# All engines of a hybrid token-mixing block in program order, its weight stages in one stream

## The chip, the cores and the metric

The kernel runs on one core of one Trainium2 chip. The metric is the device time of one execution in microseconds; runs before the change took 1920.9, 1925.97 and 1927.42 us, and their median, 1925.97 us, is the time before. Engines are named as in the profile: PE (TensorE), PEld (its weight loads), DVE (VectorE), ACT (ScalarE), POOL (GpSimd), SP (SyncE, which issues the DMAs here).

## The reference

One layer of a block over 256 latent tokens `x` and 256 context tokens `ctx` of width 2048, in float32. A conditioning vector gives six modulation rows (shift, scale, gate for the mixer and for the feed-forward part) through `w_ada`, 2048 x 12288. The mixer's input is a modulated RMSNorm; one input projection `w_in` feeds three branches and their gates:

```python
h = _rmsnorm(x, norm_mix_w) * (1 + sc_m) + sh_m       # context likewise, with its own modulation
u = h @ w_in                  # x, B, C, dt of the SSD | z | pool | Fourier | 3 gates
y = sum(gate_i * branch_i)    # box pooling, 2-D DFT, bidirectional Mamba-2 SSD
x = x + g_m * (y @ w_out)
h2 = _rmsnorm(x, norm_ffn_w) * (1 + sc_f) + sh_f
x = x + g_f * ((silu(h2 @ w_gate) * (h2 @ w_up)) @ w_down)
out = _rmsnorm(x, final_norm_w)
```

The lines above are the reference in short form. `D_FF` is 5632. The SSD runs in chunks of 128 over four groups of eight heads; `B` and the convolved columns of `x` come from 512 tokens (latent and context).

## The kernel before, in words

Float32 matrix products are made from two rounded parts of each operand, a high and a low one: `split` casts the high part on ACT (line 124) and subtracts for the low part on DVE (line 125), and `mm3` issues three PE products (lines 143 to 145, mostly 128x512). Weights stream through SBUF in stages of two k-tiles, 128x2x512 elements or 512 KB: a load into one of four `raw` buffers, a split into one of three `whi` and `wlo` pairs, then 12 products for a token-major projection. A few such stages per output, written as `proj` (line 595), make up most of the program: 8 per 512 columns of `w_in`, `w_ssd_out`, `w_out`, `w_ffn_gate` and `w_ffn_up`, 4 or 8 for `w_fourier` and `w_ffn_down`.

The first phase goes over eight row slices, `quanta`. For each, 64 PE records form 512 columns of the mixer's modulation from eight 512 KB tiles of `w_ada` (line 262), `adasb` (266) and `L269` turn them, `Am` and `Sm` (276 to 278) take them, `xnT` (287) applies them to two k-tiles of the normed tokens, and `hh`, `hl` are the parts of the result. With them go B (512 columns of `w_in`), the first 256 columns of x and dt, whose accumulators stay in PSUM over all eight slices. The other columns of x follow later (`project_x`), then C, z, the pooling input, the Fourier input, the SSD, the gates and the branches' outputs, in the order of the string `ORDER`.

The rest of the modulation (`ada_rest`, line 344: scale and shift of the feed-forward part, SC_F and SH_F, and the gates G_M, G_F) isn't made on PE but on DVE, as units: load 512 KB of `w_ada`, 128x1024, into one of the `raw` buffers, multiply by the column of `sil` and add to `adacc` (lines 353, 355). After 16 units `adacc` is split, and eight narrow products (with `strip`), a copy and a transpose, or two products with a row of ones, put it where it is used. `bg(n)` pulls these units, a set fraction of one per stage; lines 851 and 852 pull what is left of SC_F, SH_F and G_M ahead of `w_out`. G_F's units come under the SwiGLU's first stages.

What sets the order: on SP it is that of the program up to the end of the first phase, and later loads are tied to the last weight load. PE, DVE and ACT are held in program order in the input norms; PE also in the last 512 columns of `w_out`, where the norm of one token tile is made under the products of the other (`stage_h`, `norm_ffn`, `turn`). Everywhere else a list scheduler puts the instructions of an engine in order, by dependences and the program's place. Buffers in rings come free in the order of their use.

Of the kernel before, what the change touches and what calls it, by code (L numbers as in the profile page):

```python
# [64 lines left out]
WORK_AT = (0, 1, 8)  # L65
FETCH, STAGE, AT_W = 8, 1, 4

QR, QE = 4, 1
APART, APART2, TURNS0, TURNS1 = 3, 3, 1, 1
ORDER = "u P x0 c x1 u s0 x2 s1 z0 F x3 P z1 s2 p0 F z2 p1 f0 s3 z3 p2 f1 Y f2 p3 q0 f3 q1 q2 q3"  # L70
BG = {"x": 0.5, "z": 0.5, "u": 0.5, "p": 0.35, "F": 0.35, "f": 0.35, "q": 0.35, "s": 0.45}
# [3 lines left out]
def hybrid_block(ctx: ExitStack, tc, io):  # L75
# [10 lines left out]
    hp = pool("hp", 30)  # L86
    qp = pool("qp", 8)
    psp = pool("psp", 4, space=bass.MemoryType.PSUM)

    in_order = tc.manual_schedule(engines={mybir.EngineType.SP})  # L90
    in_order.__enter__()
    names = [0]
    last = [None]

    def load(dst, src):
        with tc.issue_after(last[0].ins):
            nc.sync.dma_start(dst, src)


    def nm(s):  # L100
        names[0] += 1
        return f"{s}{names[0]}"

# [5 lines left out]

    def TB(shape, nme="t"):  # L110
        return H(shape, nme=nme)
# [15 lines left out]
    def stage_raw(src, n=CH):  # L127
        raw = wp.tile([P, 2, n], F32, tag="raw", name=nm("raw"), bufs=4)
        last[0] = nc.sync.dma_start(raw, src)
        return raw  # L130

    def stage(src, n=CH, raw=None):
        raw = raw or stage_raw(src, n)
        hi = wp.tile([P, 2, n], F32R, tag="hi", name=nm("whi"), bufs=3)
        lo = wp.tile([P, 2, n], F32R, tag="lo", name=nm("wlo"), bufs=3)
        split(hi, lo, raw)
        return hi, lo

# [8 lines left out]
    # ---------------------------------------------------------------- constants  # L147
    pp = C([P, PP_N], nme="pp")
    cc = C([P, CC_N], nme="cc")
    nc.sync.dma_start(pp, io["pp"])  # L150
# [10 lines left out]
    for t in range(4):  # L161
        src = (x if t < 2 else cx)[(t % 2) * P : (t % 2 + 1) * P, :]
        halves = [H([P, 1024], nme="xt") for _ in range(2)]
        for i, h in enumerate(halves):
            nc.sync.dma_start(h, src[:, i * 1024 : (i + 1) * 1024])
        tok.append(halves)
        if t == 0:
            nc.sync.dma_start(cc, io["cc"])

    sil = C([P, 32], nme="sil")  # L170
# [4 lines left out]
    stat = H([P, KT, 32], nme="stat")  # L175
# [14 lines left out]
    # ---------------------------------------------------------------- input norms  # L190
# [3 lines left out]
    def scale_rows(t):  # L194
        r = rst[:, t : t + 1]
        ssq = C([P, 2], nme="ssq")
        for i in range(2):
            S.activation(H([P, 1024], nme="junk"), tok[t][i], AF.Square, accum_out=ssq[:, i : i + 1])
# [19 lines left out]
    with tc.manual_schedule(engines={mybir.EngineType.PE, mybir.EngineType.DVE, mybir.EngineType.Activation}):  # L218
        S.activation(C([P, 1], nme="pre"), pp[:, 0:1], AF.Square)
        S.activation(C([P, 1], nme="pre"), eps, AF.Sqrt)  # L220
        for t in range(4):
            scale_rows(t)
            if t:
                turn_in(t - 1)
        turn_in(3)
        S.copy(ones_r, ONE)
        S.copy(gt_r, GT)
        S.copy(lt_r, LT)

    # ---------------------------------------------------------------- modulation of the mixer, B and dt  # L230
# [3 lines left out]
    hl = [None] * 8  # L234

    bacc_ = [acc() for _ in range(4)]
    xacc0 = [aux() for _ in range(2)]
    dtps = aux()

    raws, w_raw = [], []  # L240

    def fetch(upto):
        while len(raws) < min(upto, 64):
            j, i = len(raws) // 8, len(raws) % 8
            raws.append(H([P, 4, 256], nme="raw"))
            nc.sync.dma_start(raws[-1], rows(w_ada, 4 * (i % 4), 4, i // 4 * D + j * 256, 256))

    def modulation(j, work):
        ps = aux()

        def units(i):
            for _ in range(WORK_AT.count(i)):
                next(work, None)

        for i in range(8):
            if i == AT_W:
                w_raw.append([stage_raw(rows(w_in, 2 * j, 2, c0, n), n) for c0, n in ((B_OFF, CH), (0, 256))])
            fetch(8 * j + i + FETCH)
            p = i % 4
            o = slice(i // 4 * 256, (i // 4 + 1) * 256)  # L260
            for k in range(4):
                T.matmul(ps[32 * k : 32 * k + 32, o], stat[:, 4 * p + k, :], raws[8 * j + i][:, k, :],  # L262
                         start=p == 0, stop=p == 3)
            units(i)
        sb = Q([P, CH], nme="adasb")
        S.copy(sb, ps)
        units(8)
        for i in range(4):
            T.matmul(ps[:, 2 * i : 2 * i + 2], sb[:, i * P : (i + 1) * P], SEL, start=True, stop=True)  # L269
# [5 lines left out]
        r = ps[:, 0:8].rearrange("p (a b) -> p a b", b=2)  # L275
# [4 lines left out]
    def modulate(b):  # L280
        hh[b] = H([P, 2, CH], F32R, nme="hh")
        hl[b] = H([P, 2, CH], F32R, nme="hl")
        for k in range(2):
            kt = 2 * b + k
            for s in range(2):
                v = xnT[b][:, k, s * 256 : (s + 1) * 256]
                V.tensor_scalar(v, v, Am[:, kt, s : s + 1], Sm[:, kt, s : s + 1], ALU.mult, ALU.add)
            split(hh[b][:, k, :], hl[b][:, k, :], xnT[b][:, k, :])

    def project_bc(b):  # L290
        """B, dt and the first columns of x of quantum b, in steps"""
        hi, lo = stage(None, CH, w_raw[b][0])
        xhi, xlo = stage(None, 256, w_raw[b][1])
        yield

        def part(out, h, l, cs):
            for k in range(2):
                kt = 2 * b + k
                mm3(out, h[:, k, cs], l[:, k, cs], hh[b][:, k, :], hl[b][:, k, :], kt == 0, kt == KT - 1)

        for ct in range(4):
            part(bacc_[ct], hi, lo, slice(ct * P, (ct + 1) * P))
            yield
        for k in range(2):
            kt = 2 * b + k
            w = dtp[kt // 8][:, kt % 8, :]
            T.matmul(dtps, w, hh[b][:, k, :], start=kt == 0, stop=False)
            T.matmul(dtps, w, hl[b][:, k, :], start=False, stop=kt == KT - 1)
        yield
        for ct in range(2):  # L310
            part(xacc0[ct], xhi, xlo, slice(ct * P, (ct + 1) * P))
            yield

    work = iter(())
    fetch(8)
    dtw = H([P, KT, 64], nme="dtw")
    nc.sync.dma_start(dtw, rows(w_in, 0, KT, DT_OFF, 64))
    # the parts of the columns of dt side by side: upper, lower
    dtp = [H([P, 8, P], F32R, nme="dtp") for _ in range(2)]
    for i in range(2):  # L320
        split(dtp[i][:, :, 0:64], dtp[i][:, :, 64:128], dtw[:, 8 * i : 8 * i + 8, :])
    for j in range(8):
        modulation(j, work)
        for _ in work:
            pass
        work = project_bc(j)
        if STAGE == 0:
            next(work)
        modulate(j)
        if STAGE == 1:  # L330
            next(work)
    for _ in work:
        pass

    in_order.__exit__(None, None, None)

    # ---------------------------------------------------------------- background: rest of the modulation
# [6 lines left out]
    def ada_rest(offs):  # L344
        for off in offs:
            for half in range(2):
                a = wp.tile([P, 1024], F32, tag="adacc", name=nm("adacc"), bufs=1)
                for kt in range(KT):
                    raw = wp.tile([P, 1024], F32, tag="raw", name=nm("raw"), bufs=4)
                    c0 = off + half * 1024  # L350
                    load(raw, w_ada[kt * P : (kt + 1) * P, c0 : c0 + 1024])
# [4 lines left out]
                    yield  # L356
                hi = wp.tile([P, 1024], F32R, tag="hi", name=nm("whi"), bufs=3)
                lo = wp.tile([P, 1024], F32R, tag="lo", name=nm("wlo"), bufs=3)
                split(hi, lo, a)
                if off in (SC_F, SH_F):  # L360
                    ps = aux()
                    for i in range(8):
# [29 lines left out]
    def bg(n):  # L392
        owed[0] += n
        while owed[0] >= 1:
            owed[0] -= 1
            next(rest, None)
# [744 lines left out]
```

## Time and profile before

| | |
|---|---|
| Runs: median (lowest to highest) | 1925.97 us (1920.9 to 1927.42) |
| Profiled execution, span | 1922.6 us |
| HBM read | 405.56 MB, 212 GB/s over the span |
| PE matmul records | 8804 |

For the profiled execution the span is the time that is listed; its distance to the median of the runs is 3.4 us. The profile has a page (busy time per engine, chain of waits, costliest groups) and views that can be asked for a window, a tile or a line. In a row of instructions, `out<-in` are the program's names, `L125` is the line of the kernel, and the number behind the bar is the busy time in us followed by the mean of one in ns. Times in the timeline are start and duration in us.

### The profile page before, as it was taken

To read this page: it belongs to the slowest core of one execution; us is meant where nothing else is said; L and a number is where in the kernel's file an instruction comes from. 1 tells how busy PE (TensorE), PEld (TensorE's weight loads), DVE (VectorE), ACT (ScalarE), POOL (GpSimd) and SP (SyncE) were. 2 spreads that over 40 slices of the span, in tenths; PEclk is the share of its full clock that TensorE was granted. 3 is DMA by queue.
4 is the path that set the end of the run, shared out by engine and by line. 5 is a ranking of instruction groups with operands and counts; after the bars stand their busy time and mean duration, and the time that the engine had idled before them with its cause. 6 is when DMAs were issued, how large, how long until landed. Compare 5 with 4: busy or idle time off the path is not lost.

```text
span 1922.6 us, 23276 instructions
## 1 busy us (share of the span) xinstructions
PE 1847.1 (96%) x8804; PEld 1483.4 (77%) x8804; DVE 1236.8 (64%) x1515; ACT 852.5 (44%) x1177; POOL 0.2 (0%) x4
## 2 busy tenths in 40 slices
PE   5999999999999999999999999999999999999998
PEld 3677886867777768777877887787788888888886
DVE  4338869695886687766656657666655555555567
ACT  5225535464464454533434544443343444433444
POOL 0000000000000000000000000000000000000000
PEclk8999999999999999999999999999999999999999
DMA  9985745454656747677777665787766666656655
GB/s 333 353 288 158 243 145 167 142 155 158 186 157 208 248 152 252 216 250 247 244 248 245 201 226 152 256 277 260 247 211 191 196 188 186 191 192 196 187 186 175
DMA packets 214081, 409.19 MB, mean 213 GB/s; under 512 B 14801, under 2 KB 51793, under 8 KB 213969
## 3 DMA queue, kind: packets, MB, share of 16 engines
q1 hardware_dynamic: 213968, 407.71, 67.1%
q8 instruction: 69, 1.13, 0.3%
q14 instruction: 44, 0.35, 0.1%
HBM read 405.56 MB, written 2.10 MB: 212 GB/s over the span
## 4 chain that ended last, share of the span: by engine, by line
PE 66%; DMA 17%; DVE 11%; issue 4%; ACT 2%; DVEq 0%; SPq 0%; ACTq 0%
PE acc L144 19%; PE acc L145 19%; PE acc L143 19%; DMA raw<-w_ada 14%; DVE wlo L125 5%; DVE adacc L355 2%; PE aux L262 1%; DVE cv L407 1%; PE aux L560 1%; DMA t<-ptab 1%; PE aux L522 1%; DMA raw<-w_in 1%; ACT whi L124 1%; PE aux L759 1%; DMA psc<-pool_scale 1%
## 5 line engine op out<-in xcount | busy, mean ns | idle before, releaser
L124 ACT CAST whi<-raw 128x1024 fp32r<-128x1024 f32 (+1 forms) x553 | 574.2, 1040 | 799.5 <-PE acc L145 554.2
L125 DVE TENSOR_TENSOR wlo<-raw,whi 128x1024 fp32r<-128x1024 f32 (+1 forms) x553 | 662.3, 1207 | 354.2 <-ACT whi L124 353.3
L144 PE MATMUL acc<-wlo,h2h 128*128 128x512 f32 x704 | 275.4, 391 | 2.5 <-DVE wlo L125 2.5
L143 PE MATMUL acc<-whi,h2h 128*128 128x512 f32 x704 | 275.0, 391 | 2.3 <-ACT h2h L124 2.3
L145 PE MATMUL acc<-whi,h2l 128*128 128x512 f32 x704 | 275.4, 391 | 0.0
L355 DVE SCALAR_TENSOR_TENSOR adacc<-raw,sil,adacc 128x1024 f32<-128x1024 f32 x120 | 154.0, 1283 | 176.1 <-DMA raw<-w_ada 175.8
L144 PE MATMUL acc<-wlo,lh 128*128 128x512 f32 x512 | 201.8, 394 | 5.4 <-DVE wlo L125 5.4
L143 PE MATMUL acc<-whi,lh 128*128 128x512 f32 x512 | 201.3, 393 | 0.0
L145 PE MATMUL acc<-whi,ll 128*128 128x512 f32 x512 | 200.6, 392 | 0.0
L144 PEld LDWEIGHTS acc<-wlo,h2h 128*128 128x128 f32 x704 | 132.4, 188 | 30.9 <-DVE wlo L125 3.8
L143 PEld LDWEIGHTS acc<-whi,h2h 128*128 128x128 f32 x704 | 132.3, 188 | 29.6 <-ACT h2h L124 2.7
L145 PEld LDWEIGHTS acc<-whi,h2l 128*128 128x128 f32 x704 | 132.5, 188 | 28.2 <-DVE h2l L125 1.3
L145 PE MATMUL acc<-whi,al 128*128 128x512 f32 x320 | 124.7, 390 | 0.0
L144 PE MATMUL acc<-wlo,ah 128*128 128x512 f32 x320 | 124.7, 390 | 0.0
L143 PE MATMUL acc<-whi,ah 128*128 128x512 f32 x320 | 124.6, 389 | 0.0
L144 PEld LDWEIGHTS acc<-wlo,lh 128*128 128x128 f32 x512 | 96.1, 188 | 29.9 <-DVE wlo L125 9.9
L145 PE MATMUL acc<-hh,wlo 128*128 128x512 f32 x288 | 113.8, 396 | 0.8 <-DVE wlo L125 0.8
L144 PE MATMUL acc<-hl,whi 128*128 128x512 f32 x288 | 114.5, 398 | 0.0
L143 PE MATMUL acc<-hh,whi 128*128 128x512 f32 x288 | 112.1, 402 | 0.9 <-ACT whi L124 0.9
L143 PEld LDWEIGHTS acc<-whi,lh 128*128 128x128 f32 x512 | 96.1, 188 | 20.7 <-issue 0.8
L145 PEld LDWEIGHTS acc<-whi,ll 128*128 128x128 f32 x512 | 96.1, 188 | 19.8 <-issue 0.2
L145 PEld LDWEIGHTS acc<-whi,al 128*128 128x128 f32 x320 | 60.1, 188 | 12.4
(294 smaller groups left out, 2467.8 us busy)
## 6 DMA issues: line engine op xcount, KB each, us to landing
raw<-w_in SPq DMA_DIRECT2D x200, 512.0 KB, 4.6
raw<-w_ada SPq DMA_DIRECT2D x192, 512.0 KB, 5.1
raw<-w_ffn_gate SPq DMA_DIRECT2D x88, 512.0 KB, 4.4
raw<-w_ffn_up SPq DMA_DIRECT2D x88, 512.0 KB, 4.4
raw<-w_ffn_down SPq DMA_DIRECT2D x88, 512.0 KB, 4.1
raw<-w_ssd_out SPq DMA_DIRECT2D x32, 512.0 KB, 4.9
raw<-w_out SPq DMA_DIRECT2D x32, 512.0 KB, 4.2
raw<-w_fourier SPq DMA_DIRECT2D x16, 512.0 KB, 4.5
```

Source lines behind the costliest of these rows:

```text
L124: S.copy(hi, src)
L125: V.tensor_tensor(lo, src, hi.bitcast(F32), ALU.subtract)
L143: T.matmul(out, ah, bh, start=first, stop=False)
L144: T.matmul(out, ah, bl, start=False, stop=False)
L145: T.matmul(out, al, bh, start=False, stop=last)
L262: T.matmul(ps[32 * k : 32 * k + 32, o], stat[:, 4 * p + k, :], raws[8 * j + i][:, k, :], start=p == 0, stop=p == 3)
L355: V.scalar_tensor_tensor(a, raw, sil[:, kt : kt + 1], a, ALU.mult, ALU.add)
L407: V.scalar_tensor_tensor(o[:, :, a:b], src[:, :, a + d : b + d], w[k], o[:, :, a:b], ALU.mult, ALU.add)
L522: T.matmul(ps, btk[:, 2 + t, :], xc[d][t], start=t == 0, stop=t == 1)
L560: T.matmul(seg, m, rh, start=n == 0, stop=n == 3)
L759: T.matmul(ps[:, k, :], u_pool[c][:, t, cc_ * P : (cc_ + 1) * P], tb[:, i, t, :], start=t == 0, stop=t == 1)
```

## The change

All engines now issue in program order (`tc.manual_schedule()` without a list). The program first lists `Stage`s, one for each 512 KB of weights with a function for its products, and `stream` then walks through them: loads are issued up to seven stages ahead, splits up to two, then come the stage's products, and behind them segments of side work, taken from generators in `beside` until the stage's `room` (1.45 us by the program's own cost figures) is used. `need` runs a generator to its end on the spot.

```diff
+LEAD, RAWS, PARTS = 2, 5, 3
+HS, QS = 28, 15
...
+    def need(*keys):
+
+        for key in keys:
+            while key not in ended:
+                step(next(e for e in beside if e[0] == key))
+
+    def stream():
+        while at["run"] < len(stages):
+            i = at["run"]
+            st = stages[i]
+            load_upto(i + LEAD + RAWS)
+            split_upto(i + LEAD + 1)
+            if st.first:
+                st.first()
+            st.mm(st.parts)
+            room = st.room
+            for entry in list(beside):
+                while room > 0.25:
+                    cost = step(entry)
+                    room -= abs(cost)
+                    if cost >= 0:
+                        break
+            for f in st.after:
+                f()
+            at["run"] += 1
```

The first phase has three stages per slice: B and two groups of 512 columns of x. Products of x end in PSUM after each slice and are added up in SBUF by DVE. The modulation of the next slice (`ada_tile`) is spread over the groups of the B and x0 stages, and `modulate` stands at the start of x1:

```diff
+    def stage_x(j, g):
+        def mm(parts):
+            if g == 1:
+                modulate(j + 1)
+            for ct in range(4):
+                ps = aux()
+                feature(ps, parts, j, ct * P, True, True)
+                if j == 0:
+                    x_sum[g, ct] = Q([P, 2, 256], nme="xin")
+                    S.copy(x_sum[g, ct].rearrange("p a b -> p (a b)"), ps)
+                else:
+                    v = x_sum[g, ct].rearrange("p a b -> p (a b)")
+                    V.tensor_tensor(v, v, ps, ALU.add)
+                if g == 0:
+                    if ct < 3:
+                        ada_tile(j + 1, 5 + ct)
+                        fetch(j + 2, 5 + ct)
+                    else:
+                        ada_sums(j + 1)
```

`ada_rest` goes in units of 128x512 (256 KB) with three buffers of its own, 16 units per 512 columns; a unit's operation is followed by the load of the third next one. Its generators are spawned while the Fourier branch's outputs run, G_M first, then SC_F and SH_F; G_F after the last stage of `w_ffn_gate`'s first columns.

```diff
-                    raw = wp.tile([P, 1024], F32, tag="raw", name=nm("raw"), bufs=4)
+                coming.append(wp.tile([P, CH], F32, tag="araw", name=nm("araw"), bufs=3))
...
+                    ask()
+                    yield -0.65
...
+    def late2():
+        def run(*a):
+            while "G_M" not in ended:
+                yield 0.0
+            yield from ada_rest(a)
+        spawn("SF", run(SC_F, SH_F))
...
+    def start_norm():
+        need("ssd", "z0", "z1", "z2", "z3")
+        spawn("Y", norm_y(), True)
+    stages[-20].after.append(start_norm)
```

In `w_out`'s last columns (the order of `w_out`'s products stays):

```diff
+        def mm_first(p):
+            def mm(parts):
+                held.append(parts)
+                mm_pair(ps, op_m, p, parts, (0,), False, p == 7)
+                if p == 7:
+                    need("o0", "o1", "o2", "SF")
+                    residual(3, 0, ps[0])
+                    turns[0] = norm_ffn(0)
+            return mm
```

At PE, in the last 512 columns of `w_out`: `acc_8994` is the first token tile's accumulator and `acc_8995` the second's. Before, one group follows the other:

```order
L143 MATMUL acc_8994<-hhi_9111,fth_8501 128x512
L144 MATMUL acc_8994<-hlo_9112,fth_8501 128x512
L145 MATMUL acc_8994<-hhi_9111,ftl_8502 128x512
L143 MATMUL acc_8995<-hhi_9087,fth_8485 128x512
L144 MATMUL acc_8995<-hlo_9088,fth_8485 128x512
L145 MATMUL acc_8995<-hhi_9087,ftl_8486 128x512
```

Now, at the same place on PE, `acc_9113` is the first tile and `acc_9114` the second; `ahi` and `alo` are the parts of an `adacc` block, `strip` and `adasb` its way to a column:

```order
L130 MATMUL acc_9113<-hhi_9225,ftl_8531 128x512
L459 MATMUL aux_9257<-ahi_9253,strip_111 32x128
L459 MATMUL aux_9257<-alo_9254,strip_111 32x128
...
L464 MATMUL aux_9257<-cc_73,adasb_9266 128x32
L459 MATMUL aux_9324<-ahi_9320,strip_111 32x128
...
L464 MATMUL aux_9516<-cc_73,adasb_9525 128x32
L128 MATMUL acc_9114<-hhi_9177,fth_8197 128x512
L129 MATMUL acc_9114<-hlo_9178,fth_8197 128x512
```

Five blocks of nine such instructions (45) stand between the two tiles' products.

On DVE at that place, before: low parts of weights, then the residual of the first tile and its norm.

```order
L125 TENSOR_TENSOR hlo_9112<-raw_9110,hhi_9111 128x1024
L125 TENSOR_TENSOR wlo_9223<-raw_9220,whi_9222 128x1024
L125 TENSOR_TENSOR wlo_9235<-raw_9232,whi_9234 128x1024
L125 TENSOR_TENSOR wlo_9247<-raw_9244,whi_9246 128x1024
L901 TENSOR_TENSOR x_8991<-acc_8994,g_8286 128x512
```

And DVE now: the end of SC_F's last block, then the units of SH_F, up to the residual.

```order
L122 TENSOR_TENSOR hlo_9244<-raw_9175,hhi_9243 128x1024
L122 TENSOR_TENSOR alo_9254<-adacc_9001,ahi_9253 128x512
L469 TENSOR_TENSOR Af_382<-aux_9257,pp_72 128x4
L471 SCALAR_TENSOR_TENSOR Af_382<-Af_382,pp_72 128x4
L446 TENSOR_SCALAR adacc_9271<-araw_9197,sil_98 128x512
L448 SCALAR_TENSOR_TENSOR adacc_9271<-araw_9218,sil_98,adacc_9271 128x512
L448 SCALAR_TENSOR_TENSOR adacc_9271<-araw_9221,sil_98,adacc_9271 128x512
...
L448 SCALAR_TENSOR_TENSOR adacc_9469<-araw_9507,sil_98,adacc_9469 128x512
L122 TENSOR_TENSOR alo_9513<-adacc_9469,ahi_9512 128x512
L469 TENSOR_TENSOR Sf_383<-aux_9516,pp_72 128x4
L1086 TENSOR_TENSOR x_9112<-acc_9113,g_7479 128x512
```

All 64 units of SH_F (16 each of `adacc_9271` and three more blocks) now stand between the low part of the weights and the residual; on SP their loads, from the fourth on, stand in one row too.

On DVE in one slice of the first phase, before: two weight splits, the parts of the tokens, then the next modulation.

```order
L125 TENSOR_TENSOR wlo_870<-raw_794,whi_869 128x1024
L125 TENSOR_TENSOR wlo_874<-raw_796,whi_873 128x512
L125 TENSOR_TENSOR hl_860<-xnT_119,hh_859 128x512 x2
L276 TENSOR_TENSOR Sm_287<-aux_877,pp_72 128x4
L277 TENSOR_TENSOR Am_286<-aux_877,pp_72 128x4
L278 SCALAR_TENSOR_TENSOR Am_286<-Am_286,pp_72 128x4
L287 TENSOR_SCALAR xnT_120<-xnT_120,Am_286,Sm_287 128x256 x4
```

DVE now, in the stage x1 of a slice:

```order
L122 TENSOR_TENSOR wlo_723<-raw_472,whi_722 128x1024
L316 TENSOR_TENSOR Sm_127<-aux_609,pp_72 128x4
L317 TENSOR_TENSOR Am_126<-aux_609,pp_72 128x4
L318 SCALAR_TENSOR_TENSOR Am_126<-Am_126,pp_72 128x4
L325 TENSOR_SCALAR xnT_119<-xnT_119,Am_126,Sm_127 128x256 x4
L328 TENSOR_TENSOR hl_730<-xnT_119,hh_729 128x512 x2
L373 TENSOR_TENSOR xin_564<-xin_564,aux_739 128x512
L373 TENSOR_TENSOR xin_573<-xin_573,aux_747 128x512
L373 TENSOR_TENSOR xin_582<-xin_582,aux_755 128x512
L373 TENSOR_TENSOR xin_591<-xin_591,aux_763 128x512
```

The additions of the x groups, which free the groups' PSUM, stand behind the whole modulation of the next slice.

More of the change, by code (lines that the diff above doesn't have):

```diff
@@ L234, in hybrid_block, with fetch, ada_tile, ada_sums @@
     hl = [None] * 8
[L236 to L267, printed above, removed]
+    raws = {}
+    aps = {}
+    def fetch(j, i):
+        if j < 8:
+            raws[j, i] = H([P, 4, 256], nme="raw")
+            load(raws[j, i], rows(w_ada, 4 * (i % 4), 4, i // 4 * D + j * 256, 256))
+    def ada_tile(j, i):
+        if j >= 8:
+            return
+        if i == 0:
+            aps[j] = aux()
+        p = i % 4
+        o = slice(i // 4 * 256, (i // 4 + 1) * 256)
+        for k in range(4):
+            T.matmul(aps[j][32 * k : 32 * k + 32, o], stat[:, 4 * p + k, :], raws[j, i][:, k, :],
+                     start=p == 0, stop=p == 3)
+        if i == 7:
+            aps[j, "sb"] = Q([P, CH], nme="adasb")
+            S.copy(aps[j, "sb"], aps[j])
+    def ada_sums(j):
+        if j >= 8:
+            return
         for i in range(4):
-            T.matmul(ps[:, 2 * i : 2 * i + 2], sb[:, i * P : (i + 1) * P], SEL, start=True, stop=True)
+            T.matmul(aps[j][:, 2 * i : 2 * i + 2], aps[j, "sb"][:, i * P : (i + 1) * P], SEL, start=True, stop=True)
+    def modulate(j):
+        if j >= 8:
+            return
         k2 = slice(2 * j, 2 * j + 2)
@@ L314, in hybrid_block @@
[L314 to L331, printed above, removed]
@@ L388, in hybrid_block @@
-    rest = ada_rest((SC_F, SH_F, G_M))
-    owed = [0.0]
[L392 to L396, printed above, removed]
+                    if q % 2 == 0:
+                        dst[q] = dst[q + 1] = H([P, 2, CH], nme="g")
+                    bb = Q([P, CH], nme="bb")
+                    load(bb, io["b_ada"][off + q * CH : off + (q + 1) * CH].partition_broadcast(P))
+                    T.matmul(ps, ones_r, hi, start=True, stop=False)
@@ new lines, in begin, with run, all_ssd @@
+    def begin():
+        def run():
+            for key, gen in (("dt", decays()), ("cB", conv_b()), ("x0", conv_x(0)), ("x1", conv_x(1))):
+                yield from gen
+                ended.add(key)
+        spawn("begin", run())
+    stages[23].after.append(begin)
+    phase_c()
+    phase_x(2)
+    st_x2 = stages[-1]
+    phase_x(3)
+    st_x3 = stages[-1]
+    def all_ssd():
+        for g in range(4):
+            while not {f"x{g}", "cB", "cC", "dt"} <= ended:
+                yield 0.0
+            yield from ssd(g)
+            ended.add(f"s{g}")
@@ L1018, in hybrid_block @@
+    stages[-1].after.append(lambda: spawn("G_F", ada_rest((G_F,))))
+    done_ = 0
+    for a, b in ((0, 4), (4, 8), (8, 10)):
+        while done_ < b + 1:
+            phase_gate_up(done_)
+            done_ += 1
+        phase_down(a, b)
+    load_upto(6)
+    split_upto(1)
+    stream()
+    for e in list(beside):
+        need(e[0])
     pieces = []
```

1198 lines of the change are left out of this document (705 added, 493 removed).

## The prediction

> **What bounds the kernel now.** I read the page from its top: the span, the busy line, the clock, the chain, the costly groups.
>
> ```profile
> span 1922.6 us, 23276 instructions
> ...
> PE 1847.1 (96%) x8804; PEld 1483.4 (77%) x8804; DVE 1236.8 (64%) x1515; ACT 852.5 (44%) x1177; POOL 0.2 (0%) x4
> ...
> PE 66%; DMA 17%; DVE 11%; issue 4%; ACT 2%; DVEq 0%; SPq 0%; ACTq 0%
> ...
> L355 DVE SCALAR_TENSOR_TENSOR adacc<-raw,sil,adacc 128x1024 f32<-128x1024 f32 x120 | 154.0, 1283 | 176.1 <-DMA raw<-w_ada 175.8
> ```
>
> PE is busy 96% of the span, so all gains together are a few per cent; a stop of PE of 20 us is already 1%. The last row is the modulation's background work: 120 VectorE instructions that stood idle 176 us for their loads. Most of that is off the path now. Next come the stretches of the program.
>
> ```profile
> 42.00:146.00 104.00, 104.00 (x758) 72.83 (x759) 34.91 (x79) 24.54 (x38) 0.00 (x0) 0.98 0.99 319
> 146.00:200.00 54.00, 48.11 (x210) 38.36 (x209) 43.95 (x59) 25.49 (x40) 0.00 (x0) 0.94 0.58 172
> 200.00:1050.00 850.00, 821.56 (x3811) 655.04 (x3810) 610.81 (x764) 405.55 (x633) 0.00 (x0) 1.00 0.64 203
> ...
> 1400.00:1900.00 500.00, 500.00 (x2234) 413.36 (x2233) 279.10 (x275) 208.70 (x211) 0.00 (x0) 1.00 0.64 194
> ```
>
> After length come PE, weight loads, VectorE, ScalarE and GpSimd, then granted clock, DMA share and GB/s. The SwiGLU stretch 1400–1900 has nothing to give. Busy time hides small gaps, since a record outlasts its slot:
>
> ```profile
> 89.00 0.39 PE L144 MATMUL acc<-hl,whi 128*128 128x512 f32 x1
> 89.22 0.39 PE L145 MATMUL acc<-hh,wlo 128*128 128x512 f32 x1
> ```
>
> Products start every 0.2275 us. Going through the timeline's starts and giving each instruction the slot of its own shape, I count the time that PE loses: 47 us up to 200 (11.35 of them before its first instruction), 62.4 in 200–1050 (the row above shows 28.4 of idle there), 16.8 in 1050–1400, under 2 to 1900. That is all the change can win by order alone, and 7 us of the 62.4 lie in the 64-wide products of L572, which stay.
>
> **The price that decides: the modulation's ring.** The order pieces show 64 units of SH_F and the end of SC_F in one piece between two groups of products of w_out's last columns. In before that work is already done there:
>
> ```profile
> 1050.00:1180.00 130.00, 0.00 (x0) 0.00 (x0) 1.00 0.57 187
> ```
>
> This is the window view for adacc alone: no modulation between 1050 and 1180. What a unit costs when nothing else covers its load, the chain of waits shows:
>
> ```profile
> 1345.04 1.30 DVE adacc L355
> ...
> 1346.36 3.64 DMA raw<-w_ada
> ...
> 1350.09 1.29 DVE adacc L355
> ```
>
> Operation ends, the load into the freed buffer starts, it lands, the operation on it runs: start to start 5.05 us, of which 0.11 are handoffs. After the change a unit is 128x512, 256 KB, with three buffers: unit u+3 is loaded when unit u is done. For 256 KB another row of the same kind of chain serves, and for 128x512 a product of that shape:
>
> ```profile
> 184.58 2.84 DMA raw<-w_in
> ```
> ```profile
> L1002 DVE TENSOR_TENSOR dn<-acc,g 128x512 f32<-128x512 f32 x24 | 15.4, 683 | 0.0
> ```
>
> So three units take 2.84 + 0.11 + 0.68 = 3.6 us. A block of 16 units is its first operation and five such hops, 18.5 us. Its tail is serial: a ScalarE cast (0.6), a VectorE subtraction (0.68), eight narrow products on PE, a copy, a transpose, an addition; with handoffs I estimate 3.3. Four blocks make 87, the end of SC_F ahead of them 3, together 90 us. VectorE may be some 5 us ahead of PE there; PE, in program order, has 45 small instructions of this work ahead of its next products, so it loses **85**, and about 1.6 more on resuming: the clock falls after a stop, and at the start it looked like this:
>
> ```profile
> 43.74 0.63 PE L144 MATMUL acc<-hl,whi 128*128 128x512 f32 x1
> 44.17 0.63 PE L145 MATMUL acc<-hh,wlo 128*128 128x512 f32 x1
> ```
>
> 0.43 per product in place of 0.2275, for some eight of them. Together **+87**. Bounds: with 3.64 per load, as for 512 KB, 20 hops are 16 us longer, 103, and with tails of 4 in place of 3.3 they make 107. Low end: the kernel's 256 KB stores at the end,
>
> ```profile
> out<-xo SPq DMA_DIRECT2D x4, 256.0 KB, 2.2
> ```
>
> with 2.2 from issue to landing, give 20 x 0.64 = 13 less, and five tails of 2.6 another 4: 70. I take 2.84, since it is a load of that size on that queue.
>
> The Trainium skill ("DMA: Bandwidth & Descriptors", section "Anatomy of one DMA — SWDGE (gpsimd) path") fits one DMA as about 2.0 us plus its bytes at 436 GB/s, for the GpSimd path; as an estimate from that page 256 KB take 2.6, near the 2.84 here, and the sum would be 5 us smaller. It speaks against this change: halving a unit halves the smaller part only, and the rows with 3.64 and 2.84 agree.
>
> The Trainium skill ("TensorE: Matmul & The Clock Gate", section "What's actually happening") says that TensorE runs at half clock after an idle window of about 3.4 us and needs as long a busy one to come back. The spacing of 0.43 agrees; by that rule alone the restart costs 1.7, no other sum.
>
> **The first phase.** A slice (a quantum) of before, from its runs of ada products:
>
> ```profile
> 70.45 2.37 PE L262 MATMUL aux<-raw,stat 128*32 128x256 f32 x40
> ...
> 79.19 0.95 PE L269 MATMUL aux<-cc,adasb 128*128 128x2 f32 x8
> ...
> 84.97 2.37 PE L262 MATMUL aux<-raw,stat 128*32 128x256 f32 x40
> ```
>
> One slice takes 14.52 us. On PE it holds 40 products of 128x512 (9.1), 64 records of ada products at 0.06 (40 of them took 2.37), 3.8, and the sums, 0.95: 13.85, so PE is nearly full while 4.98 MB come in (eight tiles, a 512 KB and a 256 KB stage), 343 GB/s. The change puts 76 products into a slice: 17.3 + 4.75 = 22.0 us, against 5.77 MB (eight tiles, three stages) or 16.8 us at that rate. The phase stays on PE; what is moved in leaves 200–1050 unchanged in cost. Its losses: the start of before ran
>
> ```profile
> 31.51 1.38 DVE L287 TENSOR_SCALAR xnT<-xnT,Am,Sm 128x256 f32<-128x256 f32 x4
> ...
> 38.55 1.13 ACT L124 CAST hh<-xnT 128x512 fp32r<-128x512 f32 x2
> ...
> 41.87 0.80 PE L143 MATMUL acc<-hh,whi 128*128 128x512 f32 x1
> ```
>
> ScalarE cast the weights ahead of hh and waited for them. The order now has hh first: 32.9 + 1.1, the weight cast by 34.7, first product near 34.8, 23.2 lost by then. The first slice has copies behind a cast that waits for a load, and a cold clock: about 5. Then each x1 stage: VectorE has wlo, three small operations, xnT x4 and hl x2 ahead of four additions that free PSUM:
>
> ```profile
> L125 DVE TENSOR_TENSOR wlo<-raw,whi 128x1024 fp32r<-128x1024 f32 x537 | 652.0, 1223 | 354.2 <-ACT whi L124 353.3 <-PE aux L508 0.4
> ```
>
> 1.22 + 0.5 + 1.4 + 1.3 = 4.4 us, while three free buffers cover two or three groups of 1.37; I take 1.7 lost, six times, 10.2. Together 38.6 where before lost 47: **-8**. From 0 lost per stage to the full 4.4, this term runs from -18 to +8.
>
> **The middle, 200–1050.** There every product waits for its weights' two parts; the change makes the parts two stages ahead, whatever side work stands between. I leave 7 for L572, 10 for places where VectorE's lag passes the two stages, 4 for the modulation ring. One more burst stands in the order: start_norm forces three units of the SSD's last group at once, between two products. Their cost is ScalarE's:
>
> ```profile
> L557 ACT ACTIVATE rh<-cc,dah 128x128 fp32r<-128x128 f32 x128 | 41.0, 391 | 20.7 <-PE aux L560 20.6
> L566 ACT ACTIVATE W<-cbf,ddt 128x128 f32<-128x128 f32 x64 | 20.8, 392 | 1.5 <-PE aux L572 1.5
> L563 ACT ACTIVATE E<-aux 128x512 f32<-128x512 f32 x16 | 9.5, 592 | 1.6 <-PE aux L560 1.3
> ```
>
> Each unit has 8, 4 and 1 of these; 41.0/128 = 0.32 and 20.8/64 = 0.325 apiece since records overlap: 4.45, three units 13.4, with handoffs some 18, less 8 of PE's own work there: +10 (8 to 12). Sum 31 for 62.4: **-31**, bounds -45 (lag hidden) and -10.
>
> **1050–1400 and the end.** The columns of w_out now wait for the last merged piece, four subtractions (0.68) behind a wlo with transposes between: 5. I estimate 8 for the norm between w_out and the SwiGLU, whose chain is the same but for the turns' places, and 6 for G_F's ring, whose 512 KB loads held 5.05 us per unit in the chain above: 19 for 16.8, **+2**, between -10 and +10. At the end the last pieces' dlo (1.22) stand behind the two operations of a residual (1.37) that they don't need: **+3**, 0 if ScalarE's casts are later anyway. Product counts, and bytes, are unchanged; the 56 additions into x_sum (0.68 each) are the ones counted in the x1 stalls.
>
> **The sum** for the profiled span: 1922.6 - 8 - 31 + 2 + 87 + 3 = 1975.6. The median of the runs, 1925.97, is 3.4 above that span, so **1979**.
>
> **Rivals.** *A, loads land fast.* If a 256 KB load into the ring takes the 2.2 of the stores, the burst is 70 and the ring never holds a stage: two of three units of a hop of 3.0 are 2.0, under the 2.73 of a stage's 12 products. If the stages then lose nothing but L572, 200–1400 gives back 72: 1922.6 - 8 - 72 + 3 + 70 = 1915.6, as run 1919, **faster**. Each 0.1 us per load adds 2 us: below 2.25 it is faster, up to 2.8 within 0.3% (about what a measurement of this kernel can tell from no change), above that slower. For it: the stretch 1400–1900 loses nothing. Against: none of the load rows above is so short, and the SSD burst stands in the order. 10% in all, 3 of them faster and 7 within 0.3%.
>
> *B, the DMA queue paces the modulation.* A stage with two units needs 1.05 MB in 2.73 us, 384 GB/s, where the fullest window above shows 319 and the slice 343. At 343 it takes 3.06: 96 such stages (64 ahead of the burst, 32 for G_F) lose 0.33 each, **+30**, 2009. Against: by the order a block of 16 units lies over some 15 stages, 12.3 MB in 42 us, 291 GB/s, and loads run up to seven stages ahead. 20%.
>
> *C, the change does not keep PE in step:* stages lose as much as before in 200–1050 (-31 becomes 0, VectorE 610.81 busy of 850 being uneven): 2010. 5%, and priced like B.
>
> **Chances.** Forecast 65%, A 10, B 20, C 5. Range 1940 to 2015: the burst at 70 (1962) with the middle at -45 (1948) and half of the first phase's better end is 1943; at the top, 107 for the burst gives 1999, the first phase's worse end 1995, B and C 2009 and 2010, and a few us are left for two of them in part. A lies outside. Faster 0.03, same 0.07, slower 0.90.
>
> **What would show it.** In the after profile: a stretch of 80 to 95 us near the end of w_out's last columns with PE nearly idle, about 64 adacc operations, and a chain of DMA araw and DVE adacc at 3.6 per three; the clock below 1.0 behind it. A first product near 35; slices of 22 to 24 us; rh activations on the chain for some 15 us. Wrong it is if those 64 operations follow each other at 0.7 us, or if the stages of 200–1050 stretch above 2.73 where units run.

## The result

The changed kernel takes 2056.16 us (median of four runs, 2054.68 to 2058.82), beside 1923.74 us for the kernel before (also four runs): a ratio of 1.0673, 95% interval 1.0642 to 1.0705. The forecast was 1979 us, 1940 to 2015. The direction was right and the largest term was right; the sum was 77 us too low.

The page of the changed kernel, lines that answer to those of before:

```profile
span 2057.0 us, 23720 instructions
...
PE 1877.8 (91%) x8808; PEld 1493.3 (73%) x8808; DVE 1308.0 (64%) x1705; ACT 842.3 (41%) x1178; POOL 0.2 (0%) x4
...
PEclk9999999999999999999999955899999999999998
...
PE 71%; DMA 11%; DVE 11%; ACT 4%; issue 3%; SPq 0%; DVEq 0%; ACTq 0%
...
L448 DVE SCALAR_TENSOR_TENSOR adacc<-araw,sil,adacc 128x512 f32<-128x512 f32 x240 | 179.8, 749 | 83.9 <-DMA araw<-w_ada 81.0
...
L459 PE MATMUL aux<-ahi,strip 128*32 128x128 f32 x32 | 7.2, 275 | 80.0 <-ACT ahi L121 80.0
```

PE's busy share fell from 96% to 91%. The last row has the cause that was forecast: 32 narrow products of the modulation, ahead of which PE stood idle for 80 us. The clock row has its hole (5, 5, 8) at the same place. The window view by the program's stretches (start and end; length, then PE, weight loads, VectorE, ScalarE, GpSimd; clock, DMA share, GB/s):

```profile
37.00:232.00 195.00, 189.16 (x1107) 125.53 (x1108) 90.11 (x146) 46.17 (x60) 0.00 (x0) 0.99 0.70 219
232.00:369.00 137.00, 127.66 (x644) 107.78 (x643) 110.82 (x163) 64.45 (x93) 0.00 (x0) 0.95 0.33 96
369.00:1075.00 706.00, 689.02 (x3125) 548.22 (x3125) 493.00 (x656) 347.56 (x563) 0.00 (x0) 0.99 0.63 198
1075.00:1183.00 108.00, 93.74 (x394) 72.40 (x392) 71.88 (x87) 38.10 (x48) 0.00 (x0) 0.96 0.73 247
1183.00:1273.00 90.00, 6.52 (x38) 4.24 (x37) 50.30 (x73) 3.74 (x9) 0.00 (x0) 0.50 0.64 195
1273.00:1356.00 83.00, 68.92 (x299) 55.98 (x298) 51.16 (x84) 31.07 (x39) 0.00 (x0) 0.87 0.45 147
```

They are: the first phase from its first B product, the columns of x and C, the rest up to `w_out`, `w_out` up to the burst, the burst, and the norm behind it up to the SwiGLU's first transposes. In the fifth, PE works 6.5 us of 90. But PE is idle 9 us in the second, 17 in the third, and 14 in each of the fourth and the sixth as well, where the forecast had hoped for gains or for small costs.

Time that PE loses, counted as in the prediction (starts against the slot of each shape), gives the balance. The slots themselves add up to 1786 us in before and 1785 in after, so all of the difference is lost time:

| PE loses, us | forecast for after | after | before |
|---|---|---|---|
| start and first phase | 38.6 | 52.4 | 47 (to 200 us) |
| up to `w_out` | 31 | 69.3 | 62.5 |
| `w_out` up to the burst | 5 | 18.3 | 0.6 |
| the burst | 87 | 87.7 | none |
| norm, up to the SwiGLU's transposes | 8 | 23.1 | 3.6 (to 1200 us) |
| stages with G_F | 6 | 4.3 | 12.5 |
| rest and tail | 13.5 | 16.6 | 10.3 |
| sum | 189 | 272 | 136 |

### The profile page after: what moved, and what is told of

The parts are those of the page before. It is cut to its first block, busy times and chain, and to the rows that moved or that the text cites. A ratio compares the mean times of both kernels' runs of the same rounds, so it can differ in the third digit from the quotient of the medians.

```text
span 2057.0 us, 23720 instructions
## 1 busy us (share of the span) xinstructions
PE 1877.8 (91%) x8808; PEld 1493.3 (73%) x8808; DVE 1308.0 (64%) x1705; ACT 842.3 (41%) x1178; POOL 0.2 (0%) x4
## 3 DMA queue, kind: packets, MB, share of 16 engines
q8 instruction: 69, 1.13, 0.2%
## 4 chain that ended last, share of the span: by engine, by line
PE 71%; DMA 11%; DVE 11%; ACT 4%; issue 3%; SPq 0%; DVEq 0%; ACTq 0%
PE acc L128 20%; PE acc L129 20%; PE acc L130 19%; DMA araw<-w_ada 9%; DVE wlo L122 3%; DVE adacc L448 2%; ACT whi L121 2%; PE aux L295 2%; PE aux L128 1%; PE aux L129 1%; PE aux L130 1%; DVE cv L497 1%; PE aux L729 1%; PE aux L648 1%; PE aux L740 0%
## 5 line engine op out<-in xcount | busy, mean ns | idle before, releaser
L122 DVE TENSOR_TENSOR wlo<-raw,whi 128x1024 fp32r<-128x1024 f32 x544 | 664.7, 1224 | 538.4 <-ACT whi L121 535.6
L121 ACT CAST whi<-raw 128x1024 fp32r<-128x1024 f32 x544 | 570.5, 1052 | 847.6 <-PE acc L130 698.9
L128 PE MATMUL acc<-whi,lh 128*128 128x512 f32 x640 | 257.8, 403 | 0.3 <-ACT xin L831 0.3
L129 PE MATMUL acc<-wlo,lh 128*128 128x512 f32 x640 | 250.4, 391 | 2.7 <-DVE wlo L122 2.7
L130 PE MATMUL acc<-whi,ll 128*128 128x512 f32 x640 | 250.0, 391 | 0.0
L448 DVE SCALAR_TENSOR_TENSOR adacc<-araw,sil,adacc 128x512 f32<-128x512 f32 x240 | 179.8, 749 | 83.9 <-DMA araw<-w_ada 81.0
L129 PEld LDWEIGHTS acc<-wlo,lh 128*128 128x128 f32 x640 | 120.6, 188 | 29.5 <-DVE wlo L122 4.0
L128 PE MATMUL acc<-hh,whi 128*128 128x512 f32 x192 | 80.9, 422 | 10.1 <-ACT xin L831 6.5
L130 PE MATMUL acc<-hh,wlo 128*128 128x512 f32 x192 | 77.2, 402 | 0.0
L129 PE MATMUL acc<-hl,whi 128*128 128x512 f32 x192 | 76.9, 400 | 0.0
```

Source lines behind the costliest of these rows:

```text
L121: S.copy(hi, src)
L122: V.tensor_tensor(lo, src, hi.bitcast(F32), ALU.subtract)
L128: T.matmul(out, ah, bh, start=first, stop=False)
L129: T.matmul(out, ah, bl, start=False, stop=False)
L130: T.matmul(out, al, bh, start=False, stop=last)
L448: V.scalar_tensor_tensor(a, raw, sil[:, kt : kt + 1], a, ALU.mult, ALU.add)
```

## The burst, read in the chain

The chain of waits of the changed kernel between the two token tiles of `w_out`'s last columns (start, duration):

```profile
1187.24 0.76 DVE adacc L448
1188.02 2.62 DMA araw<-w_ada
...
1190.73 0.76 DVE adacc L448
1191.51 2.85 DMA araw<-w_ada
...
1202.99 0.63 ACT ahi L121
1203.64 0.70 DVE alo L122
...
1204.39 0.97 PE aux L459 x7
1205.38 0.26 ACT adasb L462
...
1205.69 0.33 PE aux L464
```

One operation frees a buffer, the load lands 2.6 to 3.1 us later (once 3.73), the operation on it follows. From the block's first operation (1183.99) to its last (1202.21) five such hops take 18.2 us, 3.64 each, where 3.6 was forecast. With its tail a block takes 22.3, and the four take 89 up to PE's next 128x512 product at 1273.04. Behind it the timeline shows slow products:

```profile
1273.63 0.63 PE L129 MATMUL acc<-hlo,fth 128*128 128x512 f32 x1
...
1277.47 0.45 PE L129 MATMUL acc<-hlo,fth 128*128 128x512 f32 x1
1277.76 0.39 PE L130 MATMUL acc<-hhi,ftl 128*128 128x512 f32 x1
```

Between these starts products come every 0.43 us. From 1273.04 to 1277.76 there are eleven, 2.2 us more than at 0.2275 each. The Trainium skill ("TensorE: Matmul & The Clock Gate", section "What's actually happening") asks for a busy window of about 3.4 us before the full clock returns. The 4.7 us here are of that size, but a good microsecond longer.

## Experiments

The theories at the start were these. *Theory 1:* SH_F's burst is a cost of its own, made by where its units stand, and three buffers set its price. *Rival 2:* 64 units cost PE about as much wherever they stand. And for the 82 us by which the table exceeds the forecast outside the burst: waits in the program order itself, which repairs at single places should show. The times that follow are spans of one profiled execution each. The kernel before, run once in each round, had spans of 1922.3, 1927.6, 1922.8 and (beside even3_free and allfix_free) 1914.7 us, so a few microseconds between runs of different rounds tell nothing by themselves; the counted losses tell where a difference lies.

**sf_early**: SC_F and SH_F begin after the last x stages, G_M behind them.

```diff
+    st_x3.after.append(lambda: spawn("SF", ada_rest((SC_F, SH_F))))
...
-            yield from ada_rest(a)
-        spawn("G_M", run(G_M))
+            while "SF" not in ended:
+                yield 0.0
+            yield from ada_rest(a)
+        spawn("G_M", run(G_M))
...
```

> SC_F and SH_F begin after the last x stages and G_M after them, so nothing of SF is left for the end of w_out. Theory 1 (the burst is a cost of its own, 87 us and some 3 us of cold clock behind it, and its 64 units fit beside other stages): span 1960 to 1972. Rival 2 (VectorE pays for 64 units wherever they stand, by late wlo): half or more comes back in 370 to 1070, span 2000 to 2040.

2019.4 us: theory 1's number missed, and the span lies in rival 2's range. But the loss isn't where rival 2 puts it. The 92 us at the last columns are gone, and 68 us are lost in one piece in `w_out`'s first columns: by the order, a run of 41 units of G_M is now forced there by `need("G_M")`. The room of the stages simply never took all units; the burst had moved. It doesn't decide between 1 and 2.

**ring6**: six buffers.

```diff
-HS, QS = 28, 15
+HS, QS = 27, 14
...
-                coming.append(wp.tile([P, CH], F32, tag="araw", name=nm("araw"), bufs=3))
+                coming.append(wp.tile([P, CH], F32, tag="araw", name=nm("araw"), bufs=6))
...
-        for _ in range(3):
+        for _ in range(6):
```

> Six buffers for the units' loads in place of three (27 and 14 buffers in the two other pools instead of 28 and 15). Theory 1 (each third unit of the burst pays landing plus operation): with six the units follow each other at VectorE's 0.76, a block takes 12 plus its tail of 4, the burst 64 in place of 90: span 2025 to 2032. Rival (the queue's rate or the tails hold the burst): it stays above 80, span 2045 to 2057.

2010.4, more than expected. What VectorE waited for in the burst (total, times, longest), first in the changed kernel from 1183 to 1273 us, then here from 1165 to 1231:

```profile
DVE adacc L448 <- DMA araw<-w_ada: 28.4, 38, 1.8
```

```profile
DVE adacc L448 <- DMA araw<-w_ada: 1.8, 5, 0.7
```

The waits for landing are all but gone, and the burst loses 62 in place of 88, as theory 1 had it. The other 19 us were not expected: PE loses 4.8 in place of 14.4 between the start of `w_ssd_out` and `w_out`, and 4.7 in place of 13.9 in `w_out` up to its held stages. There a unit that waited for its load held VectorE, and the `wlo` behind it came late. These loads are slower than the burst's. Of the unit loads, first in the burst (1183 to 1273 us), then from 1000 to 1130 us, the last number is the median time to landing:

```profile
araw<-w_ada SPq DMA_DIRECT2D x61, 256.0 KB, 2.9
```

```profile
araw<-w_ada SPq DMA_DIRECT2D x47, 256.0 KB, 4.1
```

As an estimate from these rows, a hop of three units beside weight loads takes 4.1 + 0.1 + 0.75 = 5 us, so two units take 3.3, more than the 2.73 of a stage's products; with the burst's 2.9 they would take 2.5. By that a ring of three can't keep up with two units per stage there. Six buffers also took one buffer from each of two other pools, and between the columns of C and `w_ssd_out` ring6 loses some 5 us more than the changed kernel; that is not explained.

**nounits**:

```diff
-        units = [(off, q, kt) for off in offs for q in range(4) for kt in range(KT)]
+        units = [(off, q, kt) for off in offs for q in range(4) for kt in range(1)]
...
-                for kt in range(KT):
+                for kt in range(1):
```

> Leaves out 15 of every 16 units of the modulation's second part, with their loads; the tails stay. Theory 1: the burst shrinks to four blocks of 0.5 plus 4, some 18 us, -70. If the units also make wlo late between 830 and 1170 (PE lost 24 us there), another -15: span 1970 to 1980; if those losses come from the program order itself, they stay: 1985 to 1990.

1940.7: 116 us less, and 30 below the lowest span expected. PE loses nothing at the last columns and 10.6 in place of 28.3 around the start of `w_out`. More telling is what stays: with a sixteenth of this work's units the program order still loses 155 us, more than the kernel before with all of it (136). Units and burst are not the whole cause.

**room18**: more side work per stage.

```diff
-    def __init__(self, src, n, mm, first=None, room=1.45, held=False):
+    def __init__(self, src, n, mm, first=None, room=1.8, held=False):
...
-            beside.remove(entry)
+            if entry in beside:
+                beside.remove(entry)
```

> The room for side work behind a stage is 1.8 in place of 1.45; by the order no unit is then left for the end of w_out. Theory 1 (the burst exists because the side work's room is too small, not because the engines are full): burst and cold clock gone, 90, ring waits of some 10 stay: span 1960 to 1970. Rival 2 (VectorE is full; more side work per stage makes wlo late): 1985 to 2010.

2058.2, outside both ranges: no burst and no gain. The loss is now 61.5 in `w_ssd_out`'s stages, 35.8 in `w_out`'s and 20.7 under G_F. The chain there:

```profile
1050.66 3.54 DMA araw<-w_ada
...
1054.30 0.76 DVE adacc L449
...
1055.09 0.76 DVE adacc L449
...
1055.87 0.76 DVE adacc L449
...
1056.65 4.80 DMA araw<-w_ada
```

Three units per stage are a whole turn of a ring of three: each stage pays one landing on VectorE, and its `wlo` with it. A landing takes 3.5 and 4.8 us here. So units that come in threes pay for the ring outside the burst too; a room of 1.8 with six buffers was not run.

**even3, even6**: SF from the last x stage on and G_M behind it, 1.1 steps per stage apart from the room; three buffers, and six.

```diff
...
+            slow = [e for e in beside if e[0] in ("SF", "G_M",)]
+            if slow:
+                owed[0] += 1.1
+                while owed[0] >= 1 and slow[0][0] not in ended:
+                    owed[0] -= 1
+                    step(slow[0])
             for entry in list(beside):
+                if entry[0] in ("SF", "G_M",):
+                    continue
...
```

> SF from the last x stage on and G_M behind it, 1.1 steps per stage whatever the room, three buffers as in the changed kernel; by the order no block is left for w_out. Theory 1 (units that come one per stage hide their landing, 3.6 us for three against 2.73 for one stage): the 92 us at the last columns go and no more than 10 come back: span 1960 to 1975. Rival 2 (a unit costs PE 0.5 us or more wherever it stands): above 2000, as in the two kernels before that moved them.

> As even3 with six buffers. Theory 1: the ring has no wait left to lose, so it gains little over even3, 0 to 10 us: span 1955 to 1970. Rival (landing still holds VectorE in even3, the wlo behind it is late): 15 to 30 us under even3.

1963.2 and 1959.1, both as theory 1 had them. Waits of VectorE's units for their loads, from the first B product to the end of `w_out`'s first tile, first in the changed kernel ahead of its burst (37 to 1183 us), then in even3 (37 to 1180):

```profile
DVE adacc L448 <- DMA araw<-w_ada: 35.2, 34, 3.0
```

```profile
DVE adacc L457 <- DMA araw<-w_ada: 5.3, 2, 4.1
```

The two that are left belong to the last units of G_M, which are still forced in `w_out` and cost some 12 us there. With three buffers and one unit per stage, the view shows no such wait for any other unit. Rival 2 falls: even3 is 22 us above nounits, 12 of them these forced units. Six buffers gain 4 us in sum: they lose less in `w_out` and under G_F, and 8 more between the columns of C and `w_ssd_out`, as in ring6. Even3 still loses 178 us against 136 in before.

**adds, splits, norm2, ssd10**: repairs at four places of the changed kernel, for the waits that are not the units'.

```diff
-            if g == 1:
-                modulate(j + 1)
             for ct in range(4):
+                if g == 1 and ct == 1:
+                    modulate(j + 1)
```

> In x1 stages the next slice's modulation stands behind the first addition, not ahead of all four. Theory 4 (PE waits 1.13 us per slice for PSUM that the late additions hold): seven waits go, span 2048 to 2051, losses of a slice 2.5 in place of 3.6. Rival (the next slice's hl becomes late instead): 2056 to 2062.

2043.2, below the range. The first phase loses 7.5 less, as expected (the rest of the 14 us is spread over the start and other stretches and is not this edit's). In the changed kernel the fourth group of each x1 stage had waited so, in the timeline:

```profile
85.40 0.39 PE L130 MATMUL aux<-hh,wlo 128*128 128x512 f32 x1
86.76 0.50 PE L128 MATMUL aux<-hh,whi 128*128 128x512 f32 x1 [0.97 <-DVE xin L373]
```

```diff
                 if p == 7:
+                    split_upto(at["run"] + 5)
                     need("o0", "o1", "o2", "SF")
```

> Before the burst, the first stages of w_ffn_gate are split as well (two more). Theory 3 (behind the burst PE waits 8.9 us for a whi cast that stands on ScalarE behind the casts of the turned tokens): the wait goes, span 2047 to 2050. Rival (PE would then wait for the turned tokens themselves): 2054 to 2058.

2056.0, the rival's range. Behind the burst 19.9 are lost in place of 23.1, but 3.7 more ahead of it. The rival's mechanism shows too. What the first products of `w_ffn_gate` waited for, first in the changed kernel (1273 to 1357 us), then here (1276 to 1357):

```profile
PE acc L128 <- ACT whi L121: 8.7, 1, 8.7
```

```profile
PE acc L128 <- ACT h2h L121: 10.5, 3, 4.6
```

The wait for the weights' cast is gone, and PE waits for the casts of the turned tokens instead.

```diff
-            turns[1] = norm_ffn(1)
-            for i in range(1, 4):
-                turns[0](i)
+            turns[0](0, True)
+            turns[0](1)
+            turns[1] = norm_ffn(1)
+            turns[0](1, True)
...
```

(`True` asks for the low part alone; the square root's table is asked for three stages earlier.)

> As splits, and the low parts of the turned tokens stand behind the next tokens' scaling on VectorE, and the square root's table is asked for three stages earlier. Theory 5 (between w_out and the SwiGLU the subtractions directly behind their casts hold VectorE, 0.65 us each, and ScalarE's cast of weights): lost from the second tile on falls from 23 to 10 to 14: span 2043 to 2048. Rival (it is VectorE's work itself): 2054 to 2058.

2050.5, between the two ranges: lost there 17.6 in place of 23.1, of which splits alone had given 3.2. So the new order by hand gave some 2, a small part of what theory 5 had expected.

```diff
-    stages[-20].after.append(start_norm)
+    stages[-10].after.append(start_norm)
```

> start_norm, which forces what is left of the SSD, comes ten stages later. Theory 6 (three units forced at once cost 16 us because nothing stands between them): they go into stages, span 2042 to 2047. Rival (the SSD is too slow for its room, and the norm of y is then late for w_ssd_out): 2054 to 2062.

2065.8, slower and above both ranges. The stretch with the SSD's forced units loses 3.3 less, but the last columns ahead of the burst lose 15.5 in place of 4.4 and G_F's stages 8.7 in place of 4.3. Room given to the SSD is taken from other side work, so this doesn't tell what the forced units cost.

**pe_sp_order**: VectorE and ScalarE go back to the list scheduler; PE and SP keep the program order.

```diff
-    ctx.enter_context(tc.manual_schedule())
+    ctx.enter_context(tc.manual_schedule(engines={mybir.EngineType.SP, mybir.EngineType.PE}))
```

> The program order of the changed kernel for PE and SP alone; VectorE and ScalarE are ordered by the list scheduler again. Theory 7 (what eats the hoped-for gain ahead of w_out and in the norm is that subtractions stand behind their casts and wait, which a scheduler fills): the burst stays at 85 to 90, other losses fall by 15 to 35: span 2022 to 2042. Rival (it is the order on PE and the loads): 2050 to 2060.

2021.4. The burst stays (84 lost), as PE's order fixes it; the norm behind it falls from 23.1 to 5.8, the end and tail by 7.5, the columns of x and C from 16.5 to 7.1. Against it stands a worse start: the first B product comes at 57.3 us in place of 37.0. Most of the gain in the columns of x and C is one wait for a copy on ScalarE, first in the changed kernel (233 to 369 us), then here (248 to 374):

```profile
PE acc L128 <- ACT xin L831: 6.8, 2, 6.5
```

```profile
PE acc L128 <- ACT xin L831: 0.5, 1, 0.5
```

The chain of the norm, first as the changed kernel has it, then here:

```profile
1286.39 1.29 DVE h L1109 x4
1287.70 0.63 ACT h2h L121
1288.35 0.69 DVE h2l L122
1289.04 1.29 DVE h L1109 x4
1290.35 0.63 ACT h2h L121
1291.00 0.69 DVE h2l L122
...
1293.62 0.95 ACT whi L121
1294.60 1.24 DVE wlo L122
```

```profile
1276.22 0.69 DVE h2l L122
1276.91 0.65 DVE h L1109 x2
...
1277.59 0.63 ACT h2h L121
...
1278.24 0.69 DVE h2l L122
1278.93 0.65 DVE h L1109 x2
```

In program order VectorE waits for each cast before it may subtract, 2.65 us per turn, and the cast of the next weights stands on ScalarE behind all of them. The scheduler scales two columns of the next turn under the cast: 2.02 us per turn. Over eight turns that is 5 of the norm's 17 us; the rest was not taken apart.

**allfix**: even6 with adds, norm2, the last merged piece asked for only ahead of the stage that reads it, and the last weights' splits ahead of the last residual. **even3_free, allfix_free**: even3 and allfix with VectorE and ScalarE free after the first B stage, so that the start stays in program order.

```diff
-            need(f"M{0}", f"M{1}", f"M{2}", f"M{3}")
+            need("M0", "M1", "M2")
...
+            if n == 0:
+                stages[-2].first = lambda: need("M3")
...
+    stages[0].after.append(lambda: hand_.__exit__(None, None, None))
```

(`hand_` is a second manual order, of VectorE and ScalarE alone, entered at the top.)

> even6 with the additions of x1 ahead (adds, -8), the norm's order (norm2, -5), the last merged piece asked for only when its k-tiles come (-5), and the last weights' splits ahead of the last residual (-3). If these terms add up: 21 under even6, 1935 to 1949. Rival (they hide one another): within 8 of even6.

> even3 with VectorE and ScalarE in program order only up to the first B stage, and in the list scheduler's order from there; PE and SP in program order throughout. Theory 7 (the rest of the lost gain, 42 us more lost than in the kernel before in spite of no burst, is the program order of VectorE and ScalarE): pe_sp_order lost some 50 less than the changed kernel outside its start, of which 10 are gone in even3 already: span 1918 to 1930. Rival 8 (it is PE's and SP's own order, fixed stage by stage): 1945 to 1963.

> allfix with VectorE and ScalarE free after the first B stage. Theory 7: the fixes of the norm and the end were in place of what the scheduler does, so only those of PE's order (x1, last merged piece) still add, 8 to 13 under even3_free: 1908 to 1920. Rival 8: 1935 to 1944.

1944.0, 1920.1 and 1897.6. The repairs add up to 15, not 21 (the end's gave nothing). Freeing the two engines gives 43 us over even3, in theory 7's range, and 46 over allfix, 10 us below its range; rival 8 falls. Against the kernel before in the same round, which was 8 us shorter for the two free ones, it is 35 and 38. PE's lost time, from even3 to even3_free: norm 21.6 to 5.4, columns of x and C 16.1 to 8.4, first phase 26.7 to 19.4, from there to `w_ssd_out` 45.3 to 36.4, end and tail 16.0 to 8.1; only the stages of `w_ssd_out` lose more, 4.8 to 15.2. With allfix's six buffers and its later last piece they lose next to nothing again in allfix_free.

**best14**, and allfix_free once more, timed: allfix_free with 1.2 steps per stage and `start_norm` at `stages[-14]`.

> allfix_free with 1.2 steps of the modulation per stage and start_norm six stages later, so that no more than one unit of the SSD is forced. If the SSD's forced units still cost their 10 to 16 us (theory 6, now without units that they displace): span 1885 to 1892, ratio to the kernel before 0.981 to 0.986. Rival (the norm of y is late instead): 1896 to 1902, ratio 0.986 to 0.990.

> allfix_free once more, timed: theory 7 with the repairs gives 17 to 25 us under the kernel before on the same chip, ratio 0.987 to 0.991; rival (one profile's luck): above 0.995.

```profile
span 1881.3 us, 23573 instructions
...
PE 1841.7 (98%) x8808; PEld 1481.2 (79%) x8808; DVE 1290.1 (69%) x1705; ACT 848.4 (45%) x1180; POOL 0.2 (0%) x4
```

This is best14's page: 1885.24 us (five runs), a ratio of 0.9778 to the kernel before, interval 0.9756 to 0.9801; allfix_free 1898.4 us, 0.9846, 0.9823 to 0.9868. Of the 14 us between their spans 5 are in the stretch with the SSD's forced units (17.7 to 12.5 lost) and 7 in `w_out` (7.9 to 0.9), where G_M now ends in time. Both are faster than the ranges expected of them. best14 differs in two numbers at once, so theory 6 is likely but not shown alone.

## Why the prediction was wrong, step by step

- **The ring and the burst (+87):** right in place, mechanism and size. 2.84 for a load was near the rows (2.6 to 3.1); ring6's 62 lies below the low bound of 70, by buffers and not by faster loads. The Trainium skill ("DMA: Bandwidth & Descriptors", section "Anatomy of one DMA — SWDGE (gpsimd) path") gives 2.6 as an estimate, the shortest rows here.
- **The step that failed** is the middle: "the change makes the parts two stages ahead, whatever side work stands between", and with it 10 for VectorE's lag and 4 for the ring. 31 lost were forecast ahead of `w_out`, 69.3 were measured, and no gain of 31 over before came. The parts were *issued* two stages ahead, but an engine in program order also waits in order. Two such waits are shown. A unit waited for its load with a `wlo` behind it: ring6 took some 10 us away in `w_ssd_out`'s stages and 9 in `w_out`. The sum had used 2.84 for a load, which holds in the burst; beside weight loads it was 4.1. And copies, casts and subtractions stood in the order in which they are written: pe_sp_order took 9 us away in the columns of x and C, and even3_free 43 over the whole kernel (7 in the first phase, 17 from there to `w_ssd_out`, whose own stages gave 10 back, 16 in the norm).
- **What that leaves open in the middle:** of the 38 us too little, ring and order explain some 19, and the forced SSD units 6. From C up to those units some 20 us are lost where 7 were forecast for L572. They stay within a few us when the units, the burst or the order of VectorE and ScalarE go (18 in pe_sp_order, 20 in best14, 25 in ring6), so they are neither of the two waits; what they are was not taken apart. even3_free, without a burst and with free engines, still loses 60 up to `w_out`. Only with the ring, the last piece and the SSD's units mended too does the loss come near the 31 of the forecast: some 45 in allfix_free, some 38 in best14.
- **The same mistake elsewhere:** `w_out` up to the burst, 18.3 for 5 (6 of them at the last merged piece, 5 forecast; most of the rest late `wlo`), and the norm, 23.1 for 8. The order of before that the text itself printed had three `wlo` of the next weights ahead of the residual; the norm's chain was not "the same but for the turns' places".
- **The first phase (-8, measured +5):** start and PSUM stalls were about right (first product 37.0 for 34.8; 1.13 for 1.7 per slice). A slice takes 25.4 us, not 23.7. What the sum lacked were PE's changes between the ada products and the others, about 0.35 us for each visit, seven visits per slice where before has three.
- **Forced SSD units (+10):** 16 lost, the place right, the size too small. When they aren't forced (ssd10, best14), 7 to 9 us are lost in the stages just behind, so some 5 are gained, not 16. **G_F:** 4.3 for 6. **End (+3):** with the tail 16.6 for 13.5.
- **Rivals:** A fell, since loads are not that fast and the changed order gave nothing back by itself. B had the right symptom for the wrong reason: stages with units did lose time, but not to the queue's rate (247 GB/s in `w_out` where 343 had been shown, and with six buffers the same bytes came in at 261 GB/s without the loss). Beside weight loads a unit's load took 4.1 us in place of the burst's 2.9. C, "stages lose as much as before", given 5%, has the size of what happened ahead of `w_out`.

## What to carry to other kernels

A forced drain of side work costs the latency of its ring, not its engine time; print where the forced pieces stand before timing anything, and spread units one per stage rather than deepen the ring. Keep program order for the engine and the queue whose order is the plan (PE and SP here), and leave the engines that serve them to the scheduler unless each cast and subtraction has been placed by hand; the hand-made order tried here (norm2) got some 2 us where the scheduler got 17. When a loss is expected to vanish by order, count the in-order waits that the new order adds, instruction behind instruction, on every engine.

## What was not expected of the hardware

A change between 32-row ada products and full ones costs PE about 0.25 us on the way back and 0.1 on the way in, in both kernels: of no account three times a slice, 2.5 us at seven times. And in room18 a hole of 90 us went and no time was gained: the landings, paid stage by stage, cost 118 us in the stages from `w_ssd_out` to G_F's, where the changed kernel with its hole had lost 125 in them.
